# SwiGLU's gate and up as seven block products instead of eight, with their sums on GpSimd and the inner layer split at the down product

## The chip, the cores and the metric

One core of a Trainium2 chip. The metric is the device time of one execution in microseconds (us); of several runs, the median. Engines: TensorE (PE; its weight loads are PEld) multiplies, VectorE (DVE), ScalarE (ACT) and GpSimd (POOL) work elementwise, SyncE (SP) issues the transfers.

## The reference

Two layers on 512 tokens of width 1024, in float32. Each layer has a SwiGLU, a mixer of parallel head groups (retention, a gated linear recurrence, a gated delta rule), a second SwiGLU and a gated per-layer embedding:

```python
def swiglu(x, w_gate, w_up, w_down):
    return (jax.nn.silu(x @ w_gate) * (x @ w_up)) @ w_down
...
    for i in range(DEPTH):
        x = layer_norm(ALPHA * x + 0.5 * swiglu(x, ffn1_w_gate[i], ffn1_w_up[i], ffn1_w_down[i]),
                       ln_ffn1_g[i], ln_ffn1_b[i])
        mix = hybrid_mixer(x, positions, w_in[i], ...)
        x = layer_norm(ALPHA * x + mix, ln_mix_g[i], ln_mix_b[i])
        ffn = 0.5 * swiglu(x, ffn2_w_gate[i], ffn2_w_up[i], ffn2_w_down[i])
        ple = jax.nn.sigmoid(x @ ple_w_gate[i]) * (p[i] @ ple_w_proj[i])
        x = layer_norm(ALPHA * x + ffn + ple, ln_ffn2_g[i], ln_ffn2_b[i])
```

`w_gate` and `w_up` are 1024 x 2816, `w_down` is 2816 x 1024. The change concerns `x @ w_gate`, `x @ w_up` and what lies around them.

## The kernel before

**Exact products from two parts.** Every dense product is made of three: an operand is split into a rounded part `hi` (fp32r, a copy on ScalarE) and the rest `lo` (a subtraction on VectorE), and hi·hi, hi·lo and lo·hi are added up in PSUM. So each tile of 128 x 128 weights costs three matmuls (`fm`, L431; `rows`, L444), each with its own weight load. The weights are split once per use (`split_to`, L394): `act` (L214, the instruction is L215) and `tt` (L232, the instruction is L233) on pieces of 1024 columns.

**Slots.** SBUF beside the constants is 40 slots of 4 KB per partition (`Slots`, L46; `NSLOT`, L24), given out and taken back in the program's order; `Halves` (L68) gives out half slots. PSUM is eight banks of 128 x 512. `load_to` (L373) brings weights in on SP's queue, 1 MB at a time, into two raw buffers.

**Order of issue.** The program is written out by a planner: `spend` and `place` (L189, L153) keep an estimated clock for each engine, side work runs as generator threads (`spawn`, L275) that `poll` (L281) steps between matmuls when the estimate says that their inputs are there. Each engine executes in the order of issue.

**SwiGLU** (`swiglu`, L571). The weights come as 22 blocks m of 128 gate and 128 up features. For each, `fm` runs 8 tiles of K x 3 matmuls of 512 tokens for the gate and the same for the up, into two banks; `evac` (L574) takes Silu on ScalarE, the product on VectorE, and splits the 128 x 512 result into hi and lo at once. In an SwiGLU that follows another one's norm (or the kernel's start; `pend`, `NSPLIT` = 2), the first two blocks run as two halves of 256 tokens (`part`, L584), so that the first halves cover the norm of the last token tiles. Then the down product: `rows` for 22 K tiles and four token tiles, the tiles (2, 3) seven K tiles behind (0, 1) (`LAG`); x and the norm follow (`norm`, L510: residual, statistics, the root on GpSimd at L497, two scalings, eight transposes on TensorE at L261, and the split of the transposed x into `xh`, `xl`).

**Around it.** `embed` (L426) multiplies x with `ple_w_gate` in two halves of two token tiles; all eight weight tiles (16 slots) are held over both halves and given back in the second; at the end of a half GpSimd adds the result to `xt` (1024 columns per tile, L1467). The second SwiGLU follows at once. At the kernel's start (L1549) x comes in eight pieces of 256 KB among the first weights; `rotary_tables` (L1472) runs as a thread beside the first blocks.

Of the kernel before, what the change touches and what calls it, by code (L numbers as in the profile page):

```python
# [22 lines left out]
NSPLIT = 2  # L23
NSLOT = 40  # L24
# [10 lines left out]
# columns of the constant table  # L35
# [6 lines left out]
# columns of the vectors of one layer  # L42
# [3 lines left out]
class Slots:  # L46
    """Equal pieces of memory, each given out and taken back by the kernel."""
# [20 lines left out]
class Halves:  # L68
    """Half slots: two tensors of 2 KB per partition in one slot."""
# [38 lines left out]
def tile_trunk(ctx: ExitStack, tc: tile.TileContext, a, out):  # L108
# [3 lines left out]
    rpool = ctx.enter_context(tc.tile_pool(name="raw", bufs=2))  # L112
# [40 lines left out]
    def place(e, t, ns):  # L153
        """The end of work of ns that can begin at t."""
# [67 lines left out]
    def either(ns_v, ns_g):  # L222
        """The vector engine or GpSimd, whichever is done first."""
# [31 lines left out]
    def pmm(out, lhsT, rhs, ns, start=True, stop=True):  # L255
        """A product of side work."""
# [45 lines left out]
    def mm(out, lhsT, rhs, start, stop, ns):  # L302
        nc.tensor.matmul(out=out, lhsT=lhsT, rhs=rhs, start=start, stop=stop)  # L303
# [35 lines left out]
    jobs = []  # L339

    def job(src, parts):
        """src: a load of up to 8 KB per partition; parts: (first column, columns) of its units."""
        jobs.append((src, parts))

    def add_gu(l, w):
        for m in range(MT):
            job(w[l, m], [(0, 1024), (1024, 1024)])

    def add_rows(w, n, order=None):
        for c in order or range(n // 2):  # L350
            job(w[c * 256:(c + 1) * 256, :].rearrange("(j p) d -> p j d", p=128), [(0, 1024), (1024, 1024)])

    for l in range(L):
        add_gu(l, a["wgu1"])
        add_rows(a["ffn1_w_down"][l], MT)
        job(a["win_tm"][l][:, 0:1608], [(0, 804), (804, 804)])
        job(a["win_tm"][l][:, 1608:2144], [(0, 536)])
        for c in range(12):
            job(a["win_fm"][l, c], [(0, 1024), (1024, 1024)])
# [3 lines left out]
        add_gu(l, a["wgu2"])  # L363
        add_rows(a["ffn2_w_down"][l], MT)

    order = [(j, i) for j, (_, parts) in enumerate(jobs) for i in range(len(parts))]
# [3 lines left out]
    raws = {}  # L370
    stock = deque()

    def load_to(j):  # L373
        while st["loaded"] <= min(j, len(jobs) - 1):
            src, parts = jobs[st["loaded"]]
            n = parts[-1][0] + parts[-1][1]
            r = rpool.tile([128, 2048], F32, tag="raw", name="raw")
            dst = r[:, 0:n]
            if len(src.shape) == 3:
                dst = dst.rearrange("p (j d) -> p j d", j=src.shape[1])  # L380
            if st["loaded"] == 0:
                for c0, c1, kps in ((0, 512, (1,)), (512, 1024, (2, 3)), (1024, 2048, ())):
                    nc.sync.dma_start(out=dst[:, c0:c1], in_=src[:, c0:c1])
                    for kp in kps:
                        load_x(kp, 0)
            else:
                nc.sync.dma_start(out=dst, in_=src)
            raws[st["loaded"]] = r
# [1276 lines left out]
```

## Time and profile before

| | us |
|---|---|
| median of 3 runs | 2192.9 (2189.72 to 2200.47) |
| profiled execution, span from first to last instruction | 2196.0 |
| TensorE busy | 2170.8 |
| VectorE, ScalarE, GpSimd busy | 1081.6, 741.1, 221.1 |

The profiled execution's time is its span; the page gives nothing around it. A row of a table of groups names the source line, the engine, the operation, what is written and read (`s` a slot, `p` a PSUM bank, `raw` a raw buffer) with shapes, the count, the busy time, the mean length and the idle time of the engine before these instructions. Matmuls overlap in the profile, so their mean length is more than what one costs in a row. A row of a table of stretches gives the length of the stretch and each engine's busy time in it.

### The profile page before, as it was taken

How to read it: one execution, taken by the hardware profiler on the slowest of the kernel's cores; microseconds unless marked ns; L12 is line 12 of the kernel's file. 1: busy time of each engine (PE TensorE's matmuls, PEld its weight loads, DVE VectorE, ACT ScalarE, POOL GpSimd, SP SyncE). 2: the span in 40 equal slices, each digit the busy share in tenths (PEclk: the TensorE clock that was granted, in tenths of full speed). 3: DMA queues.
4: the chain of work that ended last, by engine and by line, in shares of the span. 5: the costliest groups of instructions: out<-in, count | busy, mean ns of one | idle time of the engine just before them, and what ended most of it. 6: DMA issues, size and time to landing. Idle time of an engine off the chain costs nothing.

```text
span 2196.0 us, 26879 instructions
## 1 busy us (share of the span) xinstructions
PE 2170.8 (99%) x11240; PEld 1813.3 (83%) x11240; DVE 1081.6 (49%) x1769; ACT 741.1 (34%) x1152; POOL 221.1 (10%) x170
## 2 busy tenths in 40 slices
PE   8999999999999999999999999999999999999998
PEld 7888888977888888888898888888778888888887
DVE  7323336887857432332453333278878574232324
ACT  5322223555523322232232222235565143222320
POOL 1000001233311100000000000012433110000000
PEclk9999999999979999999999999999999899999999
DMA  7222342210223322233232222421102233222330
GB/s 271 96 77 77 115 135 79 76 47 20 85 87 115 115 77 77 77 114 132 80 115 81 91 79 99 142 87 58 46 21 104 68 124 107 88 85 77 115 115 39
DMA packets 40889, 202.77 MB, mean 92 GB/s; under 512 B 3904, under 2 KB 5952, under 8 KB 26560
## 3 DMA queue, kind: packets, MB, share of 16 engines
q1 hardware_dynamic: 40768, 201.06, 26.5%
q8 instruction: 88, 1.44, 0.3%
q14 instruction: 33, 0.27, 0.0%
HBM read 198.95 MB, written 2.10 MB: 92 GB/s over the span
## 4 chain that ended last, share of the span: by engine, by line
PE 89%; DVE 6%; ACT 2%; POOL 1%; issue 1%; DMA 0%; SPq 0%; DVEq 0%; POOLq 0%; ACTq 0%
PE p L303 82%; PE p L257 6%; DVE s L233 3%; DVE s L237 2%; PE p L261 1%; ACT s L215 1%; ACT L215 0%; POOL s L233 0%; POOL fs L497 0%; POOL rk L497 0%; DMA raw<-in_wgu_dram 0%; POOL rq L497 0%; DVE s L1125 0%; DVE x L237 0%; DVE sp L237 0%
## 5 line engine op out<-in xcount | busy, mean ns | idle before, releaser
L303 PE MATMUL p<-s,s 128*128 128x512 f32 (+2 forms) x9024 | 2006.9, 380 | 7.5 <-ACT s L215 7.2
L303 PEld LDWEIGHTS p<-s,s 128*128 128x128 f32 x9024 | 1619.3, 189 | 309.2 <-ACT s L215 7.8
L233 DVE TENSOR_TENSOR s<-raw,s 128x1024 fp32r<-128x1024 f32 (+2 forms) x345 | 426.3, 1243 | 640.0 <-PE p L303 297.3
L215 ACT ACTIVATE s<-raw 128x1024 fp32r<-128x1024 f32 (+2 forms) x355 | 369.3, 1051 | 786.9 <-PE p L303 654.3
L215 ACT ACTIVATE s<-p 128x256 fp32r<-128x256 f32 (+6 forms) x464 | 190.3, 454 | 337.0 <-PE p L303 166.6
L233 DVE TENSOR_TENSOR s<-s,p 128x512 f32<-128x512 f32 (+3 forms) x176 | 102.9, 589 | 270.2 <-PE p L303 246.2
L215 ACT ACTIVATE s<-s 128x512 fp32r<-128x512 f32 (+5 forms) x205 | 112.6, 555 | 254.1 <-DVE s L233 155.3
L497 POOL TENSOR_TENSOR rs<-rs,half_neg 128x1 f32<-128x1 f32 x24 | 33.9, 1412 | 1487.1 <-DVE rs L242 1487.1
L257 PE MATMUL p<-s,s 128*128 128x64 f16 (+5 forms) x1504 | 158.6, 253 | 5.1 <-DVE s L233 3.4
L233 DVE TENSOR_TENSOR s<-s,s 128x512 fp32r<-128x512 f32 (+2 forms) x141 | 92.2, 660 | 50.0 <-ACT s L215 49.5
L257 PEld LDWEIGHTS p<-s,s 128*128 128x128 f32 (+1 forms) x688 | 95.8, 206 | 20.9 <-issue 5.5
L237 DVE SCALAR_TENSOR_TENSOR s<-p,vecs,s 128x255 f32<-128x255 f32 (+4 forms) x128 | 70.2, 551 | 15.7 <-PE p L261 7.7
L233 DVE TENSOR_TENSOR s<-p,s 128x256 fp32r<-128x256 f32 (+4 forms) x124 | 53.5, 453 | 20.2 <-ACT s L215 10.3
L215 ACT ACT_TABLE_LOAD x42 | 53.9, 1283 | 5.0 <-DVE tails L248 3.6
L257 PEld LDWEIGHTS <-s 128*128 128x128 f16 x816 | 35.2, 98 | 20.0 <-issue 10.4
L233 DVE TENSOR_TENSOR s<-p,lvm 128x512 f16<-128x512 f32 x72 | 47.0, 680 | 4.1 <-PE p L257 4.1
L233 POOL TENSOR_TENSOR s<-s,cst 128x512 f32<-128x512 f32 x26 | 37.8, 1455 | 93.8 <-DVE s L233 74.2
L237 DVE SCALAR_TENSOR_TENSOR x<-p,x 128x512 f32<-128x512 f32 x48 | 31.1, 681 | 27.4 <-PE p L303 27.3
L237 DVE SCALAR_TENSOR_TENSOR x<-x,rs,s 128x1024 f32<-128x1024 f32 (+1 forms) x25 | 30.6, 1237 | 2.8 <-POOL rs L497 2.7
L261 PE MATMUL p<-cst,s 128*128 128x128 f32 x172 | 30.9, 281 | 0.8 <-DVE s L233 0.8
L215 ACT ACTIVATE s<-p,vecs 128x256 f32<-128x256 f32 (+1 forms) x48 | 27.5, 587 | 9.8 <-PE p L303 9.8
L237 DVE SCALAR_TENSOR_TENSOR x<-x,mv,s 128x1024 f32<-128x1024 f32 (+1 forms) x25 | 30.7, 1231 | 0.0
(100 smaller groups left out, 593.5 us busy)
## 6 DMA issues: line engine op xcount, KB each, us to landing
raw<-in_wgu_dram SPq DMA_DIRECT2D x87, 1024.0 KB, 4.8
raw<-in_ffn_w_down_dram SPq DMA_DIRECT2D x44, 1024.0 KB, 4.9
raw<-in_win_fm_dram SPq DMA_DIRECT2D x24, 1024.0 KB, 4.8
raw<-in_w_out_dram SPq DMA_DIRECT2D x8, 1024.0 KB, 4.9
raw<-in_ple_w_gate_dram SPq DMA_DIRECT2D x8, 1024.0 KB, 4.9
s<-in_xT_dram SPq DMA_DIRECT2D x8, 256.0 KB, 6.6
x<-in_x_dram SPq DMA_DIRECT2D x4, 512.0 KB, 6.0
s<-in_ln_ffn_g_dram SPq DMA_DIRECT2D x4, 512.0 KB, 4.2
```

The source lines that it names most:

```text
L215: nc.scalar.activation(out=out, in_=in_, func=func, **kw)
L233: (eng or nc.vector).tensor_tensor(out=out, in0=in0, in1=in1, op=op)
L237: nc.vector.scalar_tensor_tensor(out=out, in0=in0, scalar=scalar, in1=in1, op0=op0, op1=op1)
L257: nc.tensor.matmul(out=out, lhsT=lhsT, rhs=rhs, start=start, stop=stop)
L261: nc.tensor.transpose(out, in_, idn)
L303: nc.tensor.matmul(out=out, lhsT=lhsT, rhs=rhs, start=start, stop=stop)
L497: nc.gpsimd.tensor_tensor(out=dst, in0=dst, in1=e, op=POW)
```

## The change

Write x as four blocks A11, A12, A21, A22 (tokens 0 to 255 and 256 to 511; K 0 to 511 and 512 to 1023) and a weight block of 128 gate and 128 up features as B11, B12 (K 0 to 511; gate, up) and B21, B22. The eight products of 256 tokens x 512 K x 128 features become seven, of A11·B11, S1·T1, S2·T2, S4·B22, S3·T3, A12·B21 and A22·T4, where S1 to S4 are sums of blocks of x and T1 to T4 sums of blocks of weights. Each product is 4 K tiles x 3 matmuls of 256 columns. Products are added up in one PSUM area (`b`) where a running sum is wanted (B11, T2, T3, T4 in a chain) and copied out between; another area (`d`) takes T1 and then B22.

- The weight sums run on GpSimd: three of 512 columns per block in `prepare`, one after T2's split. `prepare` is called three units ahead of T1's split. `split_one` splits a unit of 512 columns; `take(AHEAD)` keeps five units split ahead in the SwiGLU.
- The sums of x: `combine` (s1, x21, x11, x12). For layer 1's first SwiGLU and the kernel's start it runs inside `swiglu`, after four products of A11 and A12 (two blocks, `GROUP`); for the second SwiGLU it runs as a thread `blocks` in the second half of `embed`, all on GpSimd, after x has been put together again from hi and lo, as soon as 14 slots are free.
- The result of a block is kept as float32 in a half slot; `split_h` splits it at the down product, one block ahead of its use.
- 38 slots; raw buffers are five of 1024 columns for two of 2048, so that loads are 512 KB.

The core of the diff (docstrings and comments that go are left out):

```diff
-NSPLIT = 2
-NSLOT = 40
+GROUP = 2
+NSLOT = 38
+NRAW = 5
+AHEAD = 5
...
+    STEADY = ("B11", "T1", "T2", "B22", "T3", "B21", "T4")
+
+    def add_gu(l, w, group):
+        first = len(loads)
         for m in range(MT):
-            job(w[l, m], [(0, 1024), (1024, 1024)])
+            blocks4 = w[l, m].rearrange("p (g k c) -> p k g c", g=2, k=2)
+            loads.append(blocks4[:, 0])
+            loads.append(blocks4[:, 1])
+        if group:
+            for m in range(group):
+                units.extend((c, first + 2 * m, 512) for c in ("B11", "B21"))
+            for c in ("T1", "T2", "T3", "B22", "T4"):
+                units.extend((c, first + 2 * m, 512) for m in range(group))
+        for m in range(group, MT):
+            units.extend((c, first + 2 * m, 512) for c in STEADY)
...
+    def load_more():
+        while st["loaded"] < len(loads) and (st["loaded"] < NRAW or readers[st["loaded"] - NRAW] == 0):
...
+    def prepare(j):
+        if j in sums:
+            return
+        ra, rb = raws[j], raws[j + 1]
+        t = sums[j] = slots.get([128, 2, 512], F32)
+        g = nc.gpsimd
+        b11, b12, b22 = ra[:, 0:512], ra[:, 512:1024], rb[:, 512:1024]
+        tt(t[:, 0, :], b12, b11, SUB, g)
+        tt(t[:, 1, :], b22, t[:, 0, :], SUB, g)
+        tt(b12, b22, b12, SUB, g)
+
+    def halve(dst, w):
+        n = w.shape[1]
+        act(dst[:, 0, 0:n], w)
+        tt(dst[:, 1, 0:n], w, f32(dst[:, 0, 0:n]), SUB)
...
+            if c == "T1":
+                prepare(j)
+            ra, rb = raws.get(j), raws.get(j + 1)
+            w = slots.get([128, 2, 512], F32R)
+            if c in ("T1", "T2", "T4"):
+                t = sums[j]
+                halve(w, t[:, int(c != "T1"), :])
+                if c == "T2":
+                    tt(t[:, 1, :], rb[:, 0:512], t[:, 1, :], SUB, nc.gpsimd)
...
+        load_more()
+        if i + 3 < len(units) and units[i + 3][0] == "T1" and units[i + 3][1] + 1 in raws and len(slots.free) > 2 + spare[0]:
+            prepare(units[i + 3][1])
...
+    def combine(eng=None):
+        g = nc.gpsimd
+        x11, x12, x21, x22 = (xr[nm] for nm in ("A11", "A12", "A21", "A22"))
+        s1 = slots.get([128, 4, 256], F32)
+        tt(s1, x21, x22, ADD, eng)
+        tt(x21, x11, x21, SUB, g)
+        split_quad("S1", s1)
+        tt(x11, s1, x11, SUB, eng)
+        slots.put(s1)
+        split_quad("S2", x11)
+        yield
+        tt(x12, x12, x11, SUB, g)
+        split_quad("S3", x21)
+        slots.put(xr.pop("A11"), xr.pop("A21"))
+        yield
+        split_quad("S4", x12)
...
+    def product(dst, w, nm, start):
+        q = quad[nm]
+        for k in range(4):
+            h, e = q[k // 2][:, k % 2, 0, :], q[k // 2][:, k % 2, 1, :]
+            c = slice(k * 128, (k + 1) * 128)
+            mm(dst, w[:, 0, c], h, start and k == 0, False, 120.0, not start)
+            mm(dst, w[:, 0, c], e, False, False, 120.0, not start)
+            mm(dst, w[:, 1, c], h, False, k == 3, 120.0, not start)
+        begin()
...
+            def run(self, nm, w):
+                x = dict(B11="A11", T1="S1", T2="S2", B22="S4", T3="S3", B21="A12", T4="A22")[nm]
+                b, d, c = self.b[:, 0:256], self.cd[:, 0:256], self.cd[:, 256:512]
+                dst = dict(B11=b, T2=b, T3=b, T4=b, T1=d, B22=d, B21=c)[nm]
+                product(dst, w, x, nm in ("B11", "T1", "B21"))
+                slots.put(w)
+                if nm == "B11":
+                    act(self.s1, b)
+                elif nm == "T1":
+                    act(self.s5, d)
+                elif nm == "T2":
+                    act(self.u2, b)
+                elif nm == "B22":
+                    tt(self.u2, d, self.u2, ADD)
+                elif nm == "T3":
+                    act(self.u3, b)
+                    tt(self.u3, self.u3, self.s5, ADD, nc.gpsimd)
+                elif nm == "B21":
+                    tt(self.s1, c, self.s1, ADD)
+                    act(self.s1, self.s1, AF.Silu)
+                else:
+                    act(self.s5, b, AF.Silu)
...
+                if len(self.done) == 7:
+                    hh = h[self.m] = halves.get(F32)
+                    tt(hh.ap[:, 0:256], self.s1, self.u2, MUL)
+                    tt(hh.ap[:, 256:512], self.s5, self.u3, MUL)
...
+            for m in range(m0):
+                us.append(Unit(m))
+                for c in ("B11", "B21"):
+                    us[m].run(c, take(AHEAD))
+            wait(pend)
+            more = combine()
+            next(more)
+            for c in ("T1", "T2", "T3", "B22", "T4"):
+                if c in ("T2", "T3"):
+                    next(more)
+                for u in us:
+                    u.run(c, take(AHEAD))
         for m in range(m0, MT):
...
+            u = Unit(m)
+            for c in STEADY:
+                u.run(c, take(AHEAD))
+        free_quads()
+        hs = {}
+
+        def split_h(m):
+            hs[m] = slots.get([128, 2, 512], F32R)
+            split_into(hs[m], slice(0, S), h[m].ap)
+            h[m].put()
...
+        split_h(0)
         for j in range(MT):
             ws[j] = take()
+            if j + 1 < MT:
+                split_h(j + 1)
             down(j, (0, 1))
...
+        def blocks():
+            while len(slots.free) < 14:
+                yield
+            for nm in ("A11", "A12", "A21", "A22"):
+                xr[nm] = slots.get([128, 4, 256], F32)
+                for i in range(2):
+                    tt(xr[nm][:, 2 * i:2 * i + 2, :], f32(quad[nm][i][:, :, 0, :]), f32(quad[nm][i][:, :, 1, :]), ADD, nc.gpsimd)
+                if nm == "A21":
+                    yield
+            yield from combine(nc.gpsimd)
+
...
             if half:
                 wait(pend)
+                mix = spawn(blocks())
...
+        wait([mix])
...
+        load_x("A11")
+        load_part(0, 0)
+        load_x("A12")
+        load_part(1, 0)
+        load_part(2, 0)
+        load_part(3, 0)
+        load_x("A21")
+        load_part(0, 1)
+        load_part(1, 1)
+        load_x("A22")
+        load_part(2, 1)
+        load_part(3, 1)
```

The norm ahead of a SwiGLU that needs blocks writes x's blocks in place of `xh`, `xl`: split (`kind="both"`, ahead of `embed`), or A11 and A12 split and all four also as float32 (`kind="blocks"`, ahead of layer 1's first SwiGLU, with a ScalarE copy of 128 x 512 out of PSUM).

## Rows read from the trace of the kernel before

**Rows 1.** Page, part 1: busy us and share of each engine.
```profile
PE 2170.8 (99%) x11240; PEld 1813.3 (83%) x11240; DVE 1081.6 (49%) x1769; ACT 741.1 (34%) x1152; POOL 221.1 (10%) x170
```

**Rows 2.** Stages: length, busy us of PE, PEld, DVE, ACT, POOL, clock, DMA share, GB/s.
```profile
0.00:346.00 346.00, 338.54 (x1568) 284.09 (x1569) 128.32 (x161) 107.85 (x136) 5.73 (x9) 1.00 0.36 125
346.00:655.00 309.00, 303.98 (x2063) 255.41 (x2062) 240.22 (x524) 148.53 (x294) 87.40 (x69) 0.96 0.19 65
...
745.00:1101.00 356.00, 356.00 (x1580) 294.84 (x1579) 123.84 (x140) 96.01 (x117) 4.44 (x4) 1.00 0.28 97
```

**Rows 3.** Groups from 60 to 260 us, gate and up: busy us, mean ns, idle before.
```profile
L303 PE MATMUL p<-s,s 128*128 128x512 f32 x884 | 200.5, 389 | 0.0
...
L233 DVE TENSOR_TENSOR s<-raw,s 128x1024 fp32r<-128x1024 f32 x35 | 42.9, 1225 | 69.9 <-PE p L303 35.2 <-ACT s L215 19.4 <-issue 14.4
...
L233 DVE TENSOR_TENSOR s<-s,s 128x512 fp32r<-128x512 f32 x18 | 12.4, 689 | 8.2 <-ACT s L215 8.2
...
L215 ACT ACTIVATE s<-s 128x512 fp32r<-128x512 f32 x18 | 11.3, 630 | 23.4 <-DVE s L233 23.4
```

**Rows 4.** Groups from 15 to 33 us, weight loads of matmuls of 256 columns.
```profile
L303 PEld LDWEIGHTS p<-s,s 128*128 128x128 f32 x151 | 18.2, 192 | 0.0
```

**Rows 5.** Groups of the whole run, TensorE: matmuls of the dense products.
```profile
L303 PE MATMUL p<-s,s 128*128 128x512 f32 x7872 | 1858.1, 394 | 0.0
L303 PE MATMUL p<-s,s 128*128 128x256 f32 x960 | 124.9, 288 | 7.5 <-ACT s L215 7.2 <-DVE s L233 0.2
```

**Rows 6.** Groups of the whole run, VectorE and ScalarE, operations of 256 columns.
```profile
L233 DVE TENSOR_TENSOR s<-s,s 128x256 fp32r<-128x256 f32 x28 | 11.8, 421 | 4.9 <-ACT s L215 4.5
...
L233 DVE TENSOR_TENSOR s<-p,s 128x256 f32<-128x256 f32 x24 | 9.6, 410 | 0.0
...
L215 ACT ACTIVATE s<-p 128x256 f32<-128x256 f32 x76 | 27.0, 382 | 37.0 <-PE p L261 22.6 <-PE p L303 9.4 <-DVE ab L248 5.0
```

**Rows 7.** Groups of the whole run, GpSimd sums.
```profile
L233 POOL TENSOR_TENSOR x<-x,s 128x1024 f32<-128x1024 f32 x8 | 19.1, 2405 | 84.7 <-DVE s L237 84.7
...
L233 POOL TENSOR_TENSOR s<-s,s 128x512 f32<-128x512 f32 x10 | 14.6, 1461 | 24.0 <-ACT s L215 16.9 <-DVE s L233 7.1
```

**Rows 8.** Page, part 6: the loads of gate and up, KB each, us to landing.
```profile
raw<-in_wgu_dram SPq DMA_DIRECT2D x87, 1024.0 KB, 4.8
```

**Rows 9.** Timeline at 740 us: start, length, GpSimd and VectorE.
```profile
740.30 4.77 POOL L233 TENSOR_TENSOR x<-x,s 128x1024 f32<-128x1024 f32 x2 [22.41 <-DVE s L237]
742.75 3.41 DVE L233 TENSOR_TENSOR s<-raw,s 128x1024 fp32r<-128x1024 f32 x1 [1.16 <-POOL x L233]
```

**Rows 10.** Timeline at 426 us: VectorE, then GpSimd.
```profile
425.89 0.42 DVE L233 TENSOR_TENSOR s<-s,lvm 128x512 f16<-128x512 f16 x1
...
425.92 1.53 POOL L233 TENSOR_TENSOR s<-s,cst 128x512 f32<-128x512 f32 x1 [3.45 <-DVE s L233]
```

**Rows 11.** Stretch of 10 us with the rotary tables, columns as in rows 2.
```profile
50.00:60.00 10.00, 10.00 (x45) 8.27 (x45) 8.12 (x12) 4.31 (x7) 0.00 (x0) 1.00 0.37 116
```

**Rows 12.** Stretches at the start, matmuls and weight loads of L303 alone.
```profile
6.00:10.00 4.00, 2.39 (x8) 1.58 (x8) 1.00 0.96 342
10.00:14.00 4.00, 4.00 (x19) 4.00 (x19) 1.00 1.09 391
14.00:18.00 4.00, 4.00 (x34) 4.00 (x34) 1.00 0.99 366
18.00:22.00 4.00, 4.00 (x35) 3.99 (x34) 1.00 0.52 202
```

**Rows 13.** Timeline at the start of layer 1: last tile's norm, its transposes.
```profile
1101.11 1.29 DVE L237 SCALAR_TENSOR_TENSOR x<-p,x 128x512 f32<-128x512 f32 x2
...
1109.91 1.04 PE L261 MATMUL p<-cst,x 128*128 128x128 f32 x8
```

**Rows 14.** Stretches at the end, columns as in rows 2.
```profile
2188.00:2192.00 4.00, 0.29 (x2) 0.00 (x0) 3.57 (x7) 0.00 (x0) 0.92 (x1) 0.98 0.00 0
2192.00:2196.00 4.00, 0.00 (x0) 0.00 (x0) 0.82 (x2) 0.00 (x0) 0.00 (x0) 0.50 0.34 131
```

More of the change, by code (lines that the diff above doesn't have):

```diff
@@ L370, in tile_trunk, with raw_tile @@
     raws = {}
+    sums = {}
     stock = deque()
[L373 to L388, printed above, removed]
-            st["loaded"] += 1
-            if st["loaded"] == 6:
+    def raw_tile():
+        r = rpool.tile([128, 1024], F32, tag="raw", name="raw")
+        raws[st["loaded"]] = r
+        st["loaded"] += 1
+        return r
@@ new lines, in split_one, with cost, split_to, prefetch @@
+        load_more()
+        if i + 3 < len(units) and units[i + 3][0] == "T1" and units[i + 3][1] + 1 in raws and len(slots.free) > 2 + spare[0]:
+            prepare(units[i + 3][1])
+        cur[0] = keep
+    def cost(i):
+        c = units[i][0]
+        return 2 if c in ("plain", "T1") else 1
+    def split_to(i):
+        while st["split"] <= min(i, len(units) - 1):
+            split_one()
+    def prefetch(n, keep=0):
+        while st["split"] < min(st["taken"] + n, len(units)) and len(slots.free) >= cost(st["split"]) + keep + spare[0]:
+            split_one()
@@ L423, in take @@
         clk["P"] = max(clk["P"], t + HOP)
-        if len(slots.free) >= 2 * ahead + spare[0]:
-            split_to(i + ahead)
-        return hi, lo
+        prefetch(ahead)
+        return (hi, lo) if lo is not None else hi
     xh, xl = [None] * 4, [None] * 4
@@ L549, in norm @@
         yield
-        while xh[0] is None:
+        names = [f"A{1 + t // 2}{q}" for q in (1, 2)]
+        keep_raw, parts = kind == "blocks", kind == "both" or t < 2
+        while kind == "whole" and xh[0] is None:
             if len(slots.free) >= 8:
@@ L554, in norm @@
                 yield
-        c = slice(t * 128, (t + 1) * 128)
+        while kind != "whole" and names[0] not in quad and names[0] not in xr:
+            if len(slots.free) >= 4 * parts + 2 * keep_raw:
+                for nm in names:
+                    if parts:
+                        new_quad(nm)
+                    if keep_raw:
+                        xr[nm] = slots.get([128, 4, 256], F32)
+            else:
+                yield
+        c = slice(t * 128, (t + 1) * 128) if kind == "whole" else slice(t % 2 * 128, t % 2 * 128 + 128)
         for q in range(2):
@@ L657, in swiglu @@
                     drop(m)
-                    if xh[0] is not None and len(slots.free) >= 6 and st["split"] - st["taken"] < 6:
-                        split_to(st["split"])
-            ths.append(spawn(norm(t, acc[t], 0.5, gb, out), urgent=True))
+                    if xh[0] is not None or kind != "whole" and "A11" in quad:
+                        prefetch(6, 4)
+            ths.append(spawn(norm(t, acc[t], 0.5, gb, out, kind=kind), urgent=True))
         wait(ths[0:2])
```

237 lines of the change are left out of this document (130 added, 107 removed).

## The prediction

> **What bounds the kernel now.** I began with the page's busy times: TensorE is busy 2170.8 us of 2196.0, VectorE half of it, GpSimd a tenth [rows 1]. The table by stage shows where the rest is lost [rows 2]: in the SwiGLU from 745 to 1101 us TensorE never stops, the first one loses 7.5 us at the kernel's start, a mixer 5.0 us. So TensorE's instruction stream is the time, and two things count: how long the matmuls of the gate and up products take, and whether the new work on the other engines makes TensorE wait.
>
> A matmul is priced by its pace, not by its listed mean (they overlap). 884 matmuls of 512 columns fill 200.5 us, so 0.2268 us each [rows 3]; in the stretch from 15 to 33 us, all of 256 columns, 151 weight loads fill 18.2 us, so 0.1205 us each, and weight loading is busy without a gap [rows 4]. Half the columns cost 53% of the time.
>
> **What the change removes.** The gate and up of 128 features took 48 matmuls of 512 columns, or 96 of 256 in the first two blocks of each `ln_ffn1` SwiGLU. There are 4 x 22 = 88 such blocks, 4 of them split: 84 x 48 x 0.2268 + 4 x 96 x 0.1205 = 914.5 + 46.3 = 960.8 us. The counts fit: 384 of the 960 matmuls of 256 columns and 4032 of the 7872 of 512 are these [rows 5]. A block now takes seven products of 4 x 3 matmuls of 256 columns: 84 x 0.1205 = 10.12 us, for 88 blocks 890.7 us. **Gain 70 us** (not an eighth of 960.8, which would be 120). Bounds: 70 if no product waits; the price holds as long as weights and PSUM copies come in time.
>
> **What it adds in the steady state.** Per block of 10.12 us, ScalarE: seven halvings of 512 columns at 0.63 [rows 3] and six copies or Silus of 256 columns at 0.38 [rows 6], 6.7 us. VectorE: seven subtractions at 0.69 [rows 3], two additions from PSUM and two products at about 0.42 [rows 6], 6.5 us. GpSimd: four sums of 512 columns at 1.46 [rows 7] and one of 256 at about half, 6.6 us. Each fits alone. PSUM copies of the chained bank have the next product, 1.45 us, as cover: one halving and one copy on ScalarE are 1.0 us. Weights are split five products (7.2 us) ahead, and the sums are asked for three products earlier still. On ScalarE a halving of T1 waits for GpSimd; behind it stand the copies that TensorE needs, but by that lead the sum is there. SP issues two loads of 512 KB per block for one of 1 MB; the bytes are the same and a landing takes 4.8 us [rows 8], against 10 us of lead.
>
> VectorE and GpSimd do not run freely beside each other. A VectorE subtraction of 1024 columns that began while GpSimd was adding took 3.41 us for its usual 1.23: it ended 1.09 us after GpSimd did (742.75 + 3.41 against 740.30 + 4.77) [rows 3, 9]. In the other order a GpSimd sum of 512 columns ended 1.14 us after the VectorE operation in its way (425.92 + 1.53 against 425.89 + 0.42) [rows 10]. So they take turns, and a turn is shorter than the listed duration: 1.14 us for a sum of 512, and, by halves, 0.55 for a subtraction of 512 and 0.28 for one of 256. VectorE's operations with both inputs in SBUF need 7 x 0.55 + 2 x 0.28 = 4.4 us a block, GpSimd 4 x 1.14 + 0.57 = 5.1: **9.5 us of turns in 10.12 us**. I take no loss from this in the steady state, because both queues work ahead; 0.6 us is all the room. Lower bound 0; upper bound the listed durations end to end, (7 x 0.69 + 2 x 0.42) + 6.6 = 12.3 us, 2.15 us a block.
>
> The Trainium skill (SBUF — State Buffer, Who interferes with whom) says that a VectorE instruction with two SBUF inputs and a GpSimd instruction that reads SBUF exclude each other for the whole instruction, so it speaks against sums on GpSimd. This trace agrees that the second one waits (3.41 us against 1.23). Taken with whole listed durations the rule would put 88 x 2.15 = 189 us on the sum; with the turns measured here it puts nothing.
>
> In layer 0 the rotary tables come on top while the blocks run: VectorE is busy 8.1 of 10 us there [rows 11] where a SwiGLU's mean is 3.5 (123.8 in 356 us), and GpSimd has 5.7 us of it [rows 2]. Over some 25 us that is about 12 us of VectorE beyond the blocks' own; with 0.6 us of room per block I put **4 us** on it, 0 to 10.
>
> **What it adds at the seams.** *Kernel start.* Before, TensorE runs at half pace until 14 us (19 matmuls in 4 us, then 34, though the clock column says 1.00 in both) [rows 12]; by 30 us it has done 8 + 19 + 34 + 35 and, in the last 8 us, 66 more of 256 columns, about 162. Now four products (48 matmuls) can run before A21 and A22 are in. All 4 MB of x and of two blocks' weights land by about 14 us at the 366 to 391 GB/s of these windows [rows 12]. Then come, on GpSimd in order, two blocks' sums (six, 7 us, with turns for VectorE nearer 10), the difference x21 (1024 columns, 2.4 [rows 7]), and on VectorE x11, so that S2 is split at about 30 us, with 72 matmuls done: (162 - 72) x 0.1205 = **11 us** lost, 4 to 18. *Start of layer 1.* The last tile's norm needs about 9 us from TensorE's last down matmul to its transposes (1101.1 to 1109.9) and 1 us for them [rows 13]. The cover was 96 matmuls, 11.6 us; now it is four products, 5.8 us, and behind the transposes come the raw copy (0.6), s1 on VectorE (1.2) and the halving of S1 (0.6): T1 begins some 12.9 us after the down, a wait of 7 us. S2 waits for GpSimd's x21 and VectorE's x11 behind s1, another 2. An idle TensorE loses its clock: after the last matmul the granted clock drops from 2.4 to 1.2 GHz (0.50) within 4 us [rows 14], and at the start the half pace lasted 8 us from the first matmul; 3 us for that. **12 us**, 4 to 18. *Start of the second SwiGLU, twice.* Thread `blocks` needs 14 free slots; eight hold the quads, 16 the gate weights, so it starts at about the fourth of eight weight tiles of the second half, 16.3 us before the embedding's last matmul (4 x 12 + 24 matmuls at 0.2268). GpSimd then has eight additions of 512 and s1, x21, x11 (2.4 each), 17 us, and then, in its queue, the two `xt` additions of 2.4 that wait for the embedding's end, ahead of x12. S4 is halved 9 us after the embedding's end, when TensorE has had B11, T1, T2 (4.3 us): a wait of 5 us, 6 with the clock. **12 us** for both, 0 to 24. *Start of the down product, four times.* The first block's split of h stands behind the last Silu in ScalarE's queue: 0.4 + 0.6 and hand-overs, 1.4 us in which TensorE has nothing else. **6 us**, 0 to 10. Later splits (0.63 and 0.69 per 2.72 us of matmuls) lie beside them.
>
> *Mixer.* 38 slots for 40, and loads cut finer. No row prices a slot; the two mixers' idle 10 us [rows 2] could vanish or double. I take 0.
>
> **Sum.** -70 + 4 + 11 + 12 + 12 + 6 = -25 us: 2196.0 - 25 = 2171 in the profiled execution. The page gives no time around its span; the median of the runs, 2192.9, lies 3 below it, so I predict 2168.
>
> **Rivals.** *The seams are covered after all* (the planner starts the sums earlier, so that half or more of the 41 us at the seams is hidden): 2126 to 2148, about 2140. For it: at each seam the sums are asked for as soon as their inputs exist; against it: the 2.4 us sums of 1024 columns stand in one queue [rows 7]. *VectorE and GpSimd's turns become the bound.* A block has 14 turns, so 0.044 us lost at each hand-over uses up the room; from there TensorE waits in every block. If each turn costs as much as the listed duration exceeds the turn, 0.69 - 0.55 = 0.14 us, a block takes 9.5 + 14 x 0.14 = 11.5 us, 1.34 more: 88 x 1.34 = 118, so 2168 + 118 = 2286, slower. This is also where the skill's rule would lead. For it: the blocked operations [rows 9, 10]; against: the turns measured there already contain a hand-over. *The seams cost their upper bounds and the mixer loses its 10 us:* the upper bounds are 10 + 18 + 18 + 24 + 10 = 80 against the 45 taken, so 2168 + 35 + 10 = 2213 at most, 2190 half-way: no change that can be measured.
>
> **How the numbers follow.** Forecast 0.58, covered seams 0.14, turns bind 0.14, seams at their upper bounds 0.14. A change within 0.5% (11 us, 2182 to 2204) can't be told from none. The forecast's own range is 2150 to 2190, with a tenth of it above 2182. Faster: 0.58 x 0.9 + 0.14 = about 0.65; same: 0.06 and half of the last rival and a little of the turns, 0.15; slower: 0.20. The range leaves out the turns' far end and the best of the covered seams: 2130 to 2208.
>
> **What would show it.** In the changed profile: matmuls of 256 columns at 0.12 us in the steady blocks, with no idle TensorE between 100 and 230 us and a block every 10.1 us; GpSimd 50 to 80% busy in the gate and up stages; TensorE idle of 5 to 8 us at the start of layer 1 and of both second SwiGLUs, 1.4 us at each down product. Wrong it would be if TensorE waits for VectorE or GpSimd in every block (then the turns bind), if the seams show no idle, or if a block with no wait takes more than 10.2 us.

## The result and the profile after

The changed kernel takes 2352.02 us (median of 4 runs, 2348.9 to 2354.16) against 2195.26 for the kernel before beside it (2189.72 to 2200.47): ratio 1.0715, 95% interval 1.0689 to 1.074. It is 7% slower; I had predicted 2168. The profiled execution's span is 2350.6, so 154.6 us are to be explained.

The page's busy times, after:

```profile
PE 2163.3 (92%) x14216; PEld 1942.4 (83%) x14216; DVE 1622.4 (69%) x2486; ACT 1051.0 (45%) x2057; POOL 898.1 (38%) x644
```

TensorE's share fell from 99% to 92% [rows 1]: it now waits, and no other engine is full. Its busy time hardly fell although the matmuls became cheaper, because some of them ran at the lower clock: its mean over the execution is 0.963, before 0.988.

Where the time went: the matmuls of L305 (the dense products) come in a fixed number per stage, so the stages can be cut at the first matmul of each. Against before, the four gate and up stages take +37.8, +22.0, +24.6 and +20.6 us (105.0 in all), the two mixers with their output products +23.1 and +23.2, the embeddings +2.3, the down products +1.0. That is 154.6, rounding aside.

**The steady blocks.** Stretches of 50 us inside the first gate and up (length, busy time of PE, PEld, DVE, ACT, POOL, clock, DMA share, GB/s):

```profile
100.00:150.00 50.00, 45.33 (x369) 44.32 (x369) 39.63 (x49) 27.32 (x59) 31.88 (x24) 1.00 0.32 105
150.00:200.00 50.00, 44.37 (x361) 43.35 (x360) 36.65 (x48) 25.13 (x56) 25.95 (x20) 1.00 0.25 85
```

The clock is at its higher level (1.00) here and TensorE still stands for 4.7 and 5.6 us of 50. A block's 84 matmuls take between 10.1 us, the price that I gave, and 15.7 behind the first block of the first second-SwiGLU stage (up to 19.7 in layer 0's first stage): 24.8, 12.1, 10.1, 10.2, 14.1, 15.7, 11.7, 12.2, 10.1, 11.1 us and so on. So blocks that wait and blocks that don't stand side by side. In other stretches the clock falls too. The four gate and up stages without their first blocks (two of a first SwiGLU, one of a second), then the blocks of 14.1 and 15.7 us: TensorE's timeline with its waits, and stretches with TensorE alone (length, busy, clock, DMA share, GB/s):

```profile
51.50:289.60 238.10, 213.82 (x1682) 209.37 (x1682) 197.03 (x265) 131.64 (x275) 131.39 (x95) 0.96 0.31 99
827.60:1064.20 236.60, 220.80 (x1767) 217.03 (x1766) 173.92 (x229) 128.13 (x273) 128.99 (x95) 0.98 0.28 92
1223.60:1453.50 229.90, 210.66 (x1683) 206.80 (x1682) 173.62 (x223) 120.55 (x257) 126.81 (x93) 0.98 0.30 98
1988.00:2223.00 235.00, 219.38 (x1767) 215.51 (x1765) 173.73 (x228) 128.09 (x273) 128.82 (x95) 0.99 0.29 93
```

```profile
865.29 11.83 PE L305 MATMUL p<-s,s 128*128 128x256 f32 x84 [2.24 <-ACT s L217]
879.81 10.38 PE L305 MATMUL p<-s,s 128*128 128x256 f32 x62 [2.70 <-ACT s L217]
```

```profile
865.00:869.00 4.00, 3.71 (x18) 0.57 0.00 0
879.00:886.00 7.00, 6.19 (x29) 0.51 0.02 6
```

In these 82 blocks TensorE is idle for 74.9 us of 939.6. The missing clock (0.04 of 238 us, 0.02 of 237 and of 230, 0.01 of 235) is worth some 21 us more; that is an estimate from the clock column, as if TensorE had been busy throughout. The groups from 100 to 250 us:

```profile
L305 PE MATMUL p<-s,s 128*128 128x256 f32 x1114 | 137.4, 284 | 13.0 <-ACT s L217 11.3 <-DVE s L235 1.6
...
L235 DVE TENSOR_TENSOR s<-raw,s 128x512 fp32r<-128x512 f32 x52 | 52.3, 1016 | 12.4 <-ACT s L217 11.8
L235 POOL TENSOR_TENSOR s<-raw,s 128x512 f32<-128x512 f32 x26 | 36.3, 1397 | 25.0 <-DVE s L235 24.2
L235 DVE TENSOR_TENSOR s<-s,s 128x512 fp32r<-128x512 f32 x39 | 36.3, 934 | 15.0 <-ACT s L217 14.1
...
L217 ACT ACTIVATE s<-p 128x256 f32<-128x256 f32 x66 | 25.0, 380 | 39.3 <-DVE s L235 19.2 <-PE p L305 18.4 <-POOL s L235 1.5
L217 ACT ACTIVATE s<-s 128x512 fp32r<-128x512 f32 x39 | 24.3, 627 | 15.6 <-POOL s L235 13.9 <-PE p L305 1.7
L235 DVE TENSOR_TENSOR s<-s 128x256 f32<-128x256 f32 x27 | 23.5, 898 | 1.6 <-ACT s L217 1.6
...
L235 POOL TENSOR_TENSOR s<-raw 128x512 f32<-128x512 f32 x13 | 19.1, 1468 | 16.5 <-PE p L305 12.3 <-issue 3.6 <-DVE s L235 0.6
```

VectorE's subtractions of 512 columns last 1016 and 934 ns for 689 [rows 3], its products of 256 columns 898 for 421 [rows 6]: these are the turns with GpSimd. But TensorE names ScalarE, which is busy half of the time. The last columns say why: ScalarE's halvings of sums (`s<-s`) wait 13.9 us for GpSimd, its copies out of PSUM (`s<-p`) 19.2 us for VectorE. One such block in the timeline (start, length, engine; in brackets the engine's idle time and what ended it):

```profile
169.19 0.74 POOL L235 TENSOR_TENSOR s<-s 128x256 f32<-128x256 f32 x1 [1.72 <-ACT s L217]
...
170.21 1.42 POOL L235 TENSOR_TENSOR s<-raw 128x512 f32<-128x512 f32 x1 [0.29 <-PE p L305]
...
171.66 0.94 ACT L217 ACTIVATE s<-s 128x512 fp32r<-128x512 f32 x2 [2.03 <-POOL s L235]
171.71 1.30 POOL L235 TENSOR_TENSOR s<-raw,s 128x512 f32<-128x512 f32 x1
...
172.51 0.36 ACT L217 ACTIVATE s<-p 128x256 f32<-128x256 f32 x1
...
172.96 1.73 POOL L235 TENSOR_TENSOR raw<-raw 128x512 f32<-128x512 f32 x1
173.47 1.83 DVE L235 TENSOR_TENSOR s<-s 128x256 f32<-128x256 f32 x2
...
175.40 0.38 ACT L217 ACTIVATE s<-p 128x256 f32<-128x256 f32 x1 [2.02 <-DVE s L235]
...
175.84 2.34 PEld L305 LDWEIGHTS p<-s,s 128*128 128x128 f32 x19 [1.60 <-ACT s L217]
175.84 2.42 PE L305 MATMUL p<-s,s 128*128 128x256 f32 x18 [1.40 <-ACT s L217]
```

Read it backwards. TensorE begins T2 at 175.84, 1.40 us late, when the copy of B11 out of the chained bank has run (175.40). That copy waited 2.02 us for VectorE's two products of the block before to give back their slot; they took 1.83 us beside GpSimd's sum (172.96, 1.73). And all of it had begun late because ScalarE had stood for 2.03 us at a halving whose sum GpSimd finished at 171.63. That sum had begun only at 170.21. Ahead of it in GpSimd's queue stood an addition that had waited 1.72 us for ScalarE (169.19), and then TensorE released it: by the code it reads raw buffers, which TensorE doesn't touch, and writes a slot, which a product had to give back. It took 1.42 us, the next one 1.30. So it was late by its start and not by its length. In the group of these first sums of a block, TensorE ended 12.3 of 16.5 us of idle GpSimd. ScalarE executes in order: one halving that waits for a sum holds up every copy behind it, and TensorE waits for the copy.

**The seams.** The first second SwiGLU, from the timeline, and the clock there (only TensorE: length, busy, clock, DMA share, GB/s):

```profile
811.91 5.12 POOL L235 TENSOR_TENSOR x<-x,s 128x1024 f32<-128x1024 f32 x2 [1.82 <-DVE s L239]
...
814.28 0.63 ACT L217 ACTIVATE s<-raw 128x512 fp32r<-128x512 f32 x1 [5.13 <-POOL x L235]
814.72 5.13 DVE L235 TENSOR_TENSOR s<-raw,s 128x512 fp32r<-128x512 f32 x3
814.82 0.37 ACT L217 ACTIVATE s<-p 128x256 f32<-128x256 f32 x1
...
815.24 2.93 PE L305 MATMUL p<-s,s 128*128 128x256 f32 x12 [9.40 <-ACT s L217]
```

```profile
814.00:818.00 4.00, 2.76 (x12) 0.50 0.00 0
818.00:822.00 4.00, 2.48 (x12) 0.50 0.33 112
822.00:826.00 4.00, 4.00 (x26) 0.69 0.93 294
826.00:830.00 4.00, 4.00 (x36) 1.00 0.34 122
```

After a wait of 9.40 us the 12 matmuls of a product take 2.9 us at half clock (1.2 GHz), for 1.45. It is the block's third product, T2, that waits: 24 matmuls have run since the block began at 802.81. T2 needs the copy of B11 (814.82), and the copy stands behind a halving that waited 5.13 us for GpSimd's `xt` additions. The first block lasts 24.8 us for 10.1.

**A mixer** (layer 0 with its output product; columns as in the first stretches):

```profile
411.00:746.00 335.00, 311.21 (x2079) 262.03 (x2078) 247.10 (x528) 153.17 (x299) 87.52 (x72) 0.95 0.19 62
```

TensorE is idle for 23.8 us of it; before, 5.0 us of 309 [rows 2]. Here I had put 0.

### The profile page after: what moved, and what is told of

It reads as the page before. It is cut to its first block, busy times and chain, and to the rows that moved or that the text cites. A ratio compares the mean times of both kernels' runs of the same rounds, so it can differ in the third digit from the quotient of the medians.

```text
span 2350.6 us, 36020 instructions
## 1 busy us (share of the span) xinstructions
PE 2163.3 (92%) x14216; PEld 1942.4 (83%) x14216; DVE 1622.4 (69%) x2486; ACT 1051.0 (45%) x2057; POOL 898.1 (38%) x644
## 5 line engine op out<-in xcount | busy, mean ns | idle before, releaser
L305 PE MATMUL p<-s,s 128*128 128x256 f32 (+1 forms) x12000 | 1973.3, 324 | 127.3 <-ACT s L217 109.2
L305 PEld LDWEIGHTS p<-s,s 128*128 128x128 f32 x12000 | 1740.0, 195 | 291.3 <-ACT s L217 122.6
L235 DVE TENSOR_TENSOR s<-raw,s 128x512 fp32r<-128x512 f32 (+2 forms) x518 | 564.9, 1100 | 306.5 <-ACT s L217 183.5
L217 ACT ACTIVATE s<-raw 128x512 fp32r<-128x512 f32 (+1 forms) x530 | 401.4, 767 | 302.1 <-PE p L305 186.9
L217 ACT ACTIVATE s<-p 128x256 f32<-128x256 f32 (+4 forms) x812 | 307.7, 402 | 492.5 <-PE p L305 174.5
L217 ACT ACTIVATE s<-s 128x512 fp32r<-128x512 f32 (+3 forms) x585 | 327.3, 570 | 442.5 <-PE p L305 164.3
L235 DVE TENSOR_TENSOR s<-s,s 128x512 fp32r<-128x512 f32 (+2 forms) x437 | 381.5, 885 | 144.2 <-ACT s L217 136.0
L235 POOL TENSOR_TENSOR s<-raw,s 128x512 f32<-128x512 f32 (+1 forms) x188 | 295.4, 1571 | 292.6 <-DVE s L235 189.1
L235 POOL TENSOR_TENSOR s<-raw 128x512 f32<-128x512 f32 x88 | 128.9, 1467 | 218.8 <-PE p L305 184.9
L259 PE MATMUL p<-s,s 128*128 128x64 f16 (+6 forms) x1452 | 157.4, 258 | 29.8 <-DVE s L235 13.0
L235 POOL TENSOR_TENSOR raw<-raw 128x512 f32<-128x512 f32 x88 | 145.9, 1657 | 0.0
L235 DVE TENSOR_TENSOR s<-s 128x256 f32<-128x256 f32 x176 | 125.4, 739 | 10.1 <-ACT s L217 9.6
```

The source lines that it names most:

```text
L217: nc.scalar.activation(out=out, in_=in_, func=func, **kw)
L235: (eng or nc.vector).tensor_tensor(out=out, in0=in0, in1=in1, op=op)
```

## The experiments

Time is the median; "gate and up" and "mixers" are differences from the kernel before, summed over four and two stages, each from one profiled execution. The kernel before spreads over some 11 us from run to run, so a few us in the mixers show nothing.

**What the weight sums cost.** The first run leaves out the sums of weights: T1, T2 and T4 are split straight from B12, B22 and B21, so that work of GpSimd is missing (the calls of `prepare` go too). The second keeps them, on VectorE.

```diff
-                halve(w, t[:, int(c != "T1"), :])
+                halve(w, ra[:, 512:1024] if c == "T1" else rb[:, 512:1024] if c == "T2" else rb[:, 0:512])
```

> The four weight sums of each block are left out: T1, T2 and T4 are halved straight from B12, B22 and B21, so the gate and up values are not the reference's; products, copies, x sums and loads stay. Theory A (GpSimd's weight sums hold up ScalarE and VectorE, which work in a fixed order, and the PSUM copies behind them): a steady block takes 10.1 to 10.3 us in place of 11.3, the four gate and up stages come down by 80 to 120 us together, the time to 2235 to 2270 us; mixers stay 23 us longer each than before. Theory B (the chain through PSUM itself is too tight: a copy has only one product as cover): a block stays above 10.8 us.

```diff
-        g = nc.gpsimd
+        g = None
...
-                    tt(t[:, 1, :], rb[:, 0:512], t[:, 1, :], SUB, nc.gpsimd)
+                    tt(t[:, 1, :], rb[:, 0:512], t[:, 1, :], SUB)
```

> The weight sums run on VectorE instead of GpSimd, all else stays. VectorE then has about 6.5 + 4 x 0.69 = 9.3 us of work per block of 10.1. Theory A (turns between GpSimd and VectorE, and a sum that comes late): blocks at 10.2 to 10.6 us, the time 2260 to 2300 us. Rival (VectorE's own load becomes the bound, since it also waits for ScalarE): blocks above 11 us, 2340 us or more.

Measured: 2195.93 (ratio 1.0017) and 2226.1 (1.015). Both lie below their ranges. Gate and up: -50.4 and -18.8 for +105.0; mixers +48.4 and +45.1, as they were. Without the sums the 82 blocks behind the first ones take 10.12 us each, so 109 of the 155 us gained lie there; the other 46 lie at the first blocks, which the expectation did not count. With the sums on VectorE, 100 to 250 us:

```profile
L305 PE MATMUL p<-s,s 128*128 128x256 f32 x1236 | 149.8, 284 | 0.5 <-DVE s L235 0.5
...
L235 DVE TENSOR_TENSOR s<-raw,s 128x512 fp32r<-128x512 f32 x54 | 38.5, 716 | 9.1 <-ACT s L217 8.4
...
L217 ACT ACTIVATE s<-p 128x256 f32<-128x256 f32 x74 | 28.3, 382 | 36.3 <-PE p L305 31.3 <-DVE s L235 4.7
L217 ACT ACTIVATE s<-s 128x512 fp32r<-128x512 f32 x42 | 26.1, 626 | 7.2 <-PE p L305 5.1 <-DVE s L235 2.1
```

TensorE's idle 13.0 us became 0.5, the subtractions are back at 716 ns, and ScalarE's copies wait for TensorE, as they should. VectorE takes more work and the kernel gains 126 us: the sums were not too much work, they were in the wrong place. The Trainium skill (SBUF — State Buffer, Who interferes with whom) calls the port pair that VectorE and GpSimd share an exclusive lock. That agrees with both runs in direction; the size is the trace's. Both runs also take the late sums off ScalarE's path, so they don't tell how much was the lengthened operations and how much the late sums.

**The slot that the copies wait for.** The block's temporaries get a whole slot from the rotating stock in place of two half slots.

```diff
-                self.e = [halves.get(F32), halves.get(F32)]
+                self.e = slots.get([128, 2, 512], F32)
```

> The four temporaries of a block get a slot of their own that rotates, in place of two half slots that every block uses again at once, so that the first copy of a block no longer waits for the last product of the block before. Theory A: ScalarE still waits for the T1 sum; a block comes down by 0.3 us at most, the time by under 25 us. Rival C (that reuse is the chain): blocks at 10.3 us, the time down by 80 us or more, to 2270.

Measured: 2337.25 (1.0657). Gate and up +86.8, 18 us less. So the wait of the copies for VectorE was a small part. The rest lies with the sums on GpSimd, as the two runs before show; how it divides between ScalarE's order and the turns, no run shows.

**The mixers, first guess: the new estimate.** The change also gave `fm`'s products another price in the planner: 120 ns for 109 at 256 columns, which sets the order of the mixer. The kernel before with only that, and the changed kernel without it:

```diff
-        ns = (c1 - c0) * 0.4255
+        ns = (c1 - c0) * 0.4167 + 13.3
```

> The kernel before, with one line of the change alone: the planner's estimate of a matmul in fm, (c1 - c0) * 0.4167 + 13.3 in place of (c1 - c0) * 0.4255. Theory D (the mixers' 23 us each come from this, since it changes the order in which side work is issued): 2230 to 2245 us. Rival E (they come from 38 slots for 40 and from the loads in halves): within 10 us of 2195.

> The changed kernel with the planner's old estimate in fm ((c1 - c0) * 0.4255) and nothing else undone. If the estimate is all of the mixers' 46 us: 2305 us, each mixer with its output projection back at 309 to 312 us. If the 38 slots and finer loads are part of it, as the kernel before with the new estimate alone (31 us in its two mixers) lets me think: 2315 to 2325 us.

Measured: 2230.55 (1.0173), in the profiled execution +31 us, all of it in the mixers (+13.7 and +17.1). An estimate, with not one instruction's work changed, costs the kernel before 38 us by the medians. But taking it back gives the changed kernel only 9 us: 2343.63 (1.0686), mixers +35.4. A miss, as was the next, the old estimate together with the sums on VectorE:

> Weight sums on VectorE and the old estimate together. The two causes lie in different stages, so they should add: 2226 less 31 to 46, 2180 to 2195 us, equal to the kernel before or a little faster. If they were one cause (a planner led astray), the second would give nothing: 2226.

Measured 2220.91 (1.0125), 5 us below the run without the old estimate; mixers +39.9.

**The seams, and the slots.** On top of that run, once the differences of x on VectorE, once 40 slots with four raw buffers:

```diff
-        g = nc.gpsimd
+        g = None
         x11, x12, x21, x22 = (xr[nm] for nm in ("A11", "A12", "A21", "A22"))
...
-            yield from combine(nc.gpsimd)
+            yield from combine()
```

```diff
-NSLOT = 38
-NRAW = 5
+NSLOT = 40
+NRAW = 4
```

> As e6, and the differences of x's blocks (s1, x21, x11, x12) on VectorE too. If GpSimd's 2.4 us per 1024 columns and its queue set the seams (theory A): 12 to 25 us less than e6, 2160 to 2180. If the seams are set by transfers, the norm and the slots that the xt additions hold: under 6 us less.

> As e6 with 40 slots and four raw buffers, the same memory. If two slots are the rest of the mixers' loss: 10 to 15 us less than e6, the mixers back at 309 us. If the loads in halves are: the same as e6 or slower.

Measured: 2198.86 (1.0022) and 2200.61 (1.003). The first gains 22 us, nearly all in first blocks: those of the second SwiGLUs from 18.9 us each to 14.0 and 13.8. The second gains 20 us, 10.1 in the gate and up stages and 7.1 in the mixers, which keep +32.8: not the 309 us of the first expectation, and not nothing as in the second.

**What else the mixer feels.** Three edits of the kernel before: loads of 1024 columns into four such raw buffers, one slot fewer, and the finer loads with three buffers and one slot more.

```diff
-        jobs.append((src, parts))
+        for c0, n in parts:
+            jobs.append((src[:, c0 // 1024] if len(src.shape) == 3 else src[:, c0:c0 + n], [(0, n)]))
```

```diff
-NSLOT = 40
+NSLOT = 39
```

```diff
-NSLOT = 40
+NSLOT = 41
...
-    rpool = ctx.enter_context(tc.tile_pool(name="raw", bufs=4))
+    rpool = ctx.enter_context(tc.tile_pool(name="raw", bufs=3))
```

> The kernel before, with its weight loads cut into pieces of 1024 columns (512 KB) and four raw buffers of that size, as the changed kernel loads in the mixer; same slots, same estimate, same products. What is left in the mixers with the old estimate (16 to 19 us each) has to come from something else that the change does. Theory L, the finer loads move the order that the planner picks: both mixers with their output products +12 to +20 us each, the rest unchanged: 2220 to 2235. Rival, the loads don't matter (the mixer's loss comes with the slots or with what the change leaves in them): within 8 us of 2195.

> The kernel before, with 39 slots for 40 and nothing else changed (38 leave it without a place to go on). Theory S, the mixer is bound by free slots: one fewer costs 8 to 20 us in both mixers together, the SwiGLUs nothing: 2203 to 2215. Rival, the slots are not what the mixer waits for: within 4 us of 2195; then the remaining loss in the mixers is the order of side work that the planner picks, which any small change moves.

> The kernel before with its loads in pieces of 1024 columns (which by itself changed nothing, ratio 1.0004), three such raw buffers for four, and 41 slots for 40. Theory S, the mixers are bound by free slots throughout: each mixer with its output product 3 to 15 us shorter, 2160 to 2187. Rival O, 40 slots is only the size at which this order happens to come out well and any change of it costs: 2195 to 2235. Rival N, slots stop mattering at 40: within 6 us of 2193.

Measured: 2194.47 (1.0004), 2236.47 (1.02), 2205.41 (1.0058). Finer loads cost nothing in all (the two mixers -9.4 and +5.1 in the profiled execution). One slot fewer costs 44 us by the medians, in the profiled execution 37, 36 of them in the mixers; one more costs 11. So it isn't a bound that loosens with memory: the order at 40 slots is a good one, and the planner leaves it easily.

**The better variant.** All that had helped together: sums and differences on VectorE, 40 slots, own slot, with the old and the new estimate.

> The changed kernel with all the weight sums and the differences of x on VectorE, the old estimate for the mixer's products, 40 slots with 4 raw buffers, and a rotating slot of its own for a block's temporaries. If the three losses add up (the run with differences of x on VectorE stood 22 us below the one without, the run with 40 slots 20 below it): 2198.9 - 20 = 2179, 2172 to 2186, faster than the kernel before by about 16 us. Rival, the gains overlap (both shorten the same seams): 2186 to 2196, no change that can be measured. The steady blocks 10.1 us, gate and up of the second SwiGLUs 226 us or less each.

> The same kernel with the new estimate for the mixer's products. The estimate cost 4 to 9 us in the changed kernel and 35 in the one before. If it acts by itself: 5 to 10 us above its twin. If the mixer's order is simply sensitive to any change, the sign is open: between -10 and +20 from its twin. The gate and up stages within 2 us of the twin's.

Both take 2189.12 us (0.9982 and 0.998), 10 above what the gains add up to, and the estimate now makes no difference. Gate and up -41.8 and -40.8, mixers still +30.9 and +28.9. What was left was a rule at the end of the down product, which splits weights for the mixer ahead:

```diff
-                    if xh[0] is not None or kind != "whole" and "A11" in quad:
-                        prefetch(6, 4)
+                    if (xh[0] is not None or kind != "whole" and "A11" in quad) and len(slots.free) >= 6 and st["split"] - st["taken"] < 6:
+                        split_to(st["split"])
```

and, for the second SwiGLU's start, the two additions that stood at 811.91 above (the edit moves those of the embedding's first half too):

```diff
-                tt(xt[t], xt[t], sg[t], ADD, nc.gpsimd)
+                tt(xt[t], xt[t], sg[t], ADD)
```

> The fastest changed variant so far (sums and differences on VectorE, 40 slots, own slot, old estimate, 2189) with the rule of the kernel before for weights that are split ahead at the down product's end: one unit per product of the last tiles, with six free slots, for as many as fit at once with four kept. Theory W, this is what takes the mixer's slots at its start: the first part of each mixer back by 8 to 14 us, 2162 to 2176. Rival, it isn't: mixers within 4 us, total within 6 us of 2189.

> The fastest changed variant so far with the embedding's last two additions of 1024 columns on VectorE for GpSimd. Theory T, they block VectorE's sums at the start of the second SwiGLU (a subtraction of 512 columns took 1.9 us there): the first block there from 14.0 and 13.0 us to 11 to 12, 2 to 6 us in all, 2183 to 2187. Rival: VectorE is late by its own work, no gain or a loss: 2188 to 2194.

> Both edits together. If they act apart: the sum of the two differences within 4 us. If the order of the mixer moves with any change, the mixer's part differs from the run with the old splitting rule by more than that.

Measured: 2162.97 (0.9866), 2184.6 (0.996), and both 2153.44: ratio 0.9814, 95% interval 0.9782 to 0.9845, **41 us faster than the kernel before** and 199 faster than the changed one. That is 5 us below what the two edits add up to.

```profile
PE 2104.8 (98%) x14216; PEld 1899.9 (88%) x14216; DVE 1593.4 (74%) x2864; ACT 1053.9 (49%) x2057; POOL 324.8 (15%) x266
```

That is its page's line of busy times: TensorE is at 98% again, with 66 us less to do than before [rows 1]. With both, the mixers are at -0.9 in all and the gate and up stages at -46.8; the second SwiGLUs' first blocks take 10.1 us. The mixer of layer 0 in stretches of 80 and 76 us from equal points, without the old rule (first fence) and with it (second), columns as above:

```profile
446.00:526.00 80.00, 75.88 (x658) 60.09 (x656) 60.08 (x119) 55.18 (x118) 27.25 (x26) 0.94 0.06 19
526.00:602.00 76.00, 66.11 (x437) 53.33 (x437) 58.78 (x126) 27.16 (x53) 19.77 (x19) 0.98 0.16 55
```

```profile
447.00:527.00 80.00, 77.99 (x685) 63.82 (x684) 65.63 (x135) 39.00 (x94) 27.47 (x23) 1.00 0.12 39
527.00:603.00 76.00, 74.65 (x491) 60.08 (x489) 59.53 (x115) 49.41 (x85) 28.08 (x23) 1.00 0.19 62
```

Without the old rule, half as much is loaded in the first stretch (19 GB/s for 39). Dense products have run ahead: 487 of their matmuls fall in the 77 us before it, for 466 with the rule, and then 116 and 128 in the two stretches, for 168 and 183. So the side work has fewer of them beside it, and in the second stretch TensorE is idle for 9.9 us of 76 instead of 1.4, most of it waiting for VectorE. That the stock of split weights holds the slots there fits both tables; it wasn't measured by itself.

**Taking apart the mixers' 46 us** in the changed kernel with its sums on GpSimd: the old rule alone, then with 40 slots, four raw buffers and the old estimate.

> The changed kernel with the old rule for weights split ahead at the down product's end and nothing else changed: 38 slots, the new estimate and the sums on GpSimd stay. Theory W, the rule is the whole of the mixers' loss: both mixers with their output products within 6 us of the kernel before, 2300 to 2312. Rival M, any one of the three (the rule, the new estimate, the missing slots) is enough to bring the loss, as one slot or the estimate alone did in the kernel before: the mixers keep +30 to +46 in all, 2335 to 2352.

> The same with 40 slots, 4 raw buffers and the old estimate as well: all that the change did to the mixer's order is undone, its SwiGLUs with the sums on GpSimd stay. Both theories: mixers with their output products within 8 us of the kernel before in all; gate and up stages some 0 to 10 us shorter than in the changed kernel by the slots; 2290 to 2308.

Measured: 2348.43 (1.0696), mixers +45.3; and 2320.91 (1.0573), mixers +5.7. The rule alone gives nothing; all three back give 41 of 46 us. Rival M holds: any one of them is enough for the poor order (the estimate and one slot fewer by the runs of the kernel before, the rule by the better variant with and without it). The second run missed its range upwards since its gate and up stages lost 13 us more (+118.2). I have no shown cause; with its four raw buffers and 40 slots the first sums of a block waited 24.4 us for TensorE from 100 to 250 us, where the changed kernel's waited 12.3.

## Why the prediction was wrong

My sum was 2171 for the profiled execution, which took 2350.6: 180 us of error, in three terms (small ones, of 2 to 5 us, cancel).

**"I take no loss from this in the steady state, because both queues work ahead": 105 us, the step that failed.** Taking the first two blocks of a first SwiGLU and the first of a second as the seams, the other 82 blocks take 109 us more than 82 x 10.12, 1.33 each, where I had put 4 in all. What I got wrong is that a sum of turns below the block's time (9.5 of 10.12 us, which no run measured) means no wait. The queues' order is fixed, ScalarE's among them, and GpSimd's sums stand on ScalarE's path to the PSUM copies. I had seen that path and closed it with "by that lead the sum is there". It was not there: my lead of eight products was one in the order of issue, while on the chip the sum in the timeline began only at 170.21, behind an addition that waited for ScalarE and a slot that TensorE gave back, and ScalarE stood for it from 169.63 to 171.66. From 100 to 250 us its halvings of sums waited 13.9 us for GpSimd, and its copies 19.2 for VectorE, whose operations GpSimd lengthens. Nor is all of the 109 us a wait: TensorE is idle for 74.9, and the clock that fell after the longer waits is worth an estimated 21.

The rival "turns bind" gave 1.34 us a block, 118 in all, and "TensorE waits in every block". Its size and sign came out; that every block waits did not, since blocks of 10.1 us stand among the others and a fifth of the loss is the clock. So the agreement in size may be luck. How the waits divide between turns and late sums stays open. I gave this rival 0.14 though I had counted 6% of room over 14 hand-overs.

**"Mixer: I take 0": 46 us.** I looked at slots and loads as resources and found no row with a price. I didn't ask what sets the order there. The diff changes three inputs of the planner in that stage, its price of `fm`'s products, its slots and the rule for splitting ahead, and each alone is enough (+31 by the price in the kernel before, +36 by one slot there, about +29 by the rule in the better variant). The bound of 10 us, double the idle time shown, was no bound.

**The seams: 29 us.** At the first blocks the waits beyond 10.12 us each are 24.0 (start), 17.0 (layer 1), 14.7 and 14.9 (second SwiGLUs), 71 in all; less the 6 or so that the kernel before loses at its own start and split blocks, 64 against my 35 (11 + 12 + 12). That GpSimd's queue costs at the seams was predicted and holds. Without the weight sums the four are 11.0, 8.7, 2.3 and 2.3, though x's differences and the `xt` additions stay on GpSimd; with the weight sums on VectorE they are 24.2, 11.1, 8.8 and 8.8, with x's differences there too 14.8, 8.1, 3.9 and 3.7, and with the `xt` additions moved as well (in the variant with 40 slots) the second SwiGLUs' are nil. The path was another than mine. I had TensorE wait for S4, after B11, T1 and T2; it stopped ahead of T2, since ScalarE's copy stood behind a halving that waited for the `xt` additions. And I had left the weight sums out of GpSimd's queue there. The listed 2.4 us of a GpSimd sum of 1024 columns became 2.6 (5.12 for two), and VectorE's subtractions of 512 columns took 1.7 us for 0.69 there (5.13 for three). Of the 14.7 us of the first second SwiGLU 10.9 are idle (9.40 and 1.52), and the rest is the clock, which stayed low for some 9 us from the first matmul after the wait. Two of my sums also don't come out: eight additions at 1.46 and three at 2.4 are 18.9 us and not 17, and layer 1's parts (9, 1, 0.6, 1.2, 0.6) make 12.4 and not 12.9. For one second SwiGLU I had 6 us, an upper bound of 12, and it took 15.

**Right.** The block's price: 10.1 us wherever nothing waits; without the weight sums 1503 matmuls fill 180.5 us, 0.1201 each for my 0.1205. So was the gain of 70: that run, with no sums of weights, has gate and up at -50.4, near the 70 less the 24 us that its first blocks still wait. The start of the down product I had at 1.4 us, four times. By the way the stages are cut, that wait falls to the last block of gate and up, and these take 10.3 to 10.6 us: 0.2 to 0.5 each, and the down stages lost 1.0 us in all. Why it is less I have not tested.

## What to carry to other kernels

Where two engines exclude each other, a sum of turns just below the budget is not room: follow each shared operand to the in-order queue that consumes it, and ask what else waits behind it, and when the memory that it writes comes free. Here the same sums cost 126 us less on the busier engine. And where a planner writes the order, every input of it that a diff touches (a price, a memory size, a rule for working ahead) is a change to all stages that it orders, and needs a range of its own size; the way to test it is to apply that input alone to the kernel before.

## What was not expected of the hardware

VectorE alone carries its own work and all the sums of a block with TensorE idle for 0.5 us in 150, while VectorE and GpSimd with the same work idle it for 13.0. Waits of some 1.4 us in a block left the granted clock at 1.00 from 100 to 200 us. After waits of 2.24 and 2.70 us it stood at 0.57 and 0.51 in the stretches of 4 and 7 us that follow, and after a wait of 9.4 us it stood at 0.50 in the two stretches of 4 us from the first matmul on, at 0.69 in the third and at 1.00 in the fourth.
